# A 224-byte pad that moves h^T to the slots' place within 1024 bytes

## The chip, the core and the metric

One NeuronCore of a Trainium2 chip runs the whole program. The metric is the device time in microseconds. Three runs of the kernel before took 1566.57, 1566.58 and 1566.65 us, so the median is 1566.58 us. The engines are named as the profile names them: PE is TensorE's matmul and PEld its weight load, DVE is VectorE, ACT is ScalarE, POOL is GpSimd, SP is SyncE, which issues the transfers.

## What is computed

Two layers of a hybrid encoder over 512 tokens of width 1024, in float32. Cut to what matters here:

```
for l in range(2):
    h = rmsnorm(x, norm_pre[l])                     # 512 x 1024
    p = h @ w_in[l]                                 # 1024 x 10,400: q, k, v, gates of four mixers
    y_a, y_b, y_c, y_d = the four mixers of p       # windowed, recurrent, differential, latent attention
    g = sigmoid(p["gate"] + b_gate[l])              # 4 x 1024
    merged = sum(g_i * (y_i @ w_br_i[l]))           # four branch projections to width 1024
    x = x + rmsnorm(merged @ w_out[l], norm_post[l])
```

The product h @ w_in is by far the largest part. Its operand h is the same for all 10,400 columns.

## The kernel before

Every large product is made of three matmuls on float32r parts: each operand is split into a high part (a copy in float32r, made by ScalarE) and a low part (the rest, made by VectorE), and `mm3` (L434) issues high times high, high times low and low times high into one PSUM bank. A matmul has a stationary operand, which a weight load brings into the array, and a moving operand, which streams through it. In the profile's names a matmul `ps<-hTh,wl` has hTh moving and wl stationary.

h is transposed once per layer (L976, L977) into two tiles that hold it whole, hTh and hTl, each 128 partitions by 8 blocks by 512 tokens, that is 16,384 bytes in each partition, one block of 2048 bytes for each 128 channels. Nearly all columns of w_in go through `item_T` (L552): the weights are stationary (128 by 128), a block of hTh or hTl is moving (128 by 512 tokens). The rest goes through `item_tok` (L587) with the roles exchanged: 128 tokens of h stationary, 384, 416 or 512 columns of weights moving. The branch projections and w_out use the same functions with other tiles in the place of h (ya, yb, yc, yd and mh).

All those other tiles, the weights' parts (wh, wl) among them, are slots: 82 buffers of 2048 bytes in each partition, one pool, taken by `slot` (L380). The constants, the identity for transposes, h^T and a few small tiles lie in a pool of their own ahead of the slots, allocated one after the other in `setup` (L1708). Counted from the tiles' sizes, in bytes of each partition:

```
                    before            after
cst   (9232 B)        1152 =  1x1024+128     34144 = 33x1024+352
ident (512 B)        10400 = 10x1024+160     43392 = 42x1024+384
junk  (2048 B)       10912 = 10x1024+672     43904 = 42x1024+896
hTh   (16384 B)      13024 = 12x1024+736      1376 =  1x1024+352
hTl   (16384 B)      29408 = 28x1024+736     17760 = 17x1024+352
prm   (1024 B)       45792 = 44x1024+736     46016 = 44x1024+960
slots (82 x 2048 B)  47456 = 46x1024+352     48480 = 47x1024+352
```

A stationary piece of a slot starts 0, 512, 1024 or 1536 bytes into it. So before the change every operand pair of slots lies 0 or 512 bytes apart (counted within 1024), and every pair of h^T and a slot 384 or 896.

The order of the work is set by a planner in the kernel (`Sched`, L95, and `drive`, L1850), which keeps a modelled clock for each engine. Its rules read instruction shapes and tile names, never addresses; it prices a float32r matmul of 512 columns at 512/2400 + 0.0025 = 0.216 us (L187).

Of the kernel before, what the change touches and what calls it, by code (L numbers as in the profile page):

```python
# [9 lines left out]
F32 = mybir.dt.float32  # L10
F32R = mybir.dt.float32r
# [5 lines left out]
P = 128  # L17
# [23 lines left out]

N_SLOT = 82
N_STAGE = 4
W_FIRST = 8
BANKS = {"d": 3, "S": 2, "T": 2, "O": 1}
W_MIN = 7
# [316 lines left out]
class Trunk:  # L363
# [131 lines left out]
    def load_w(self, upto):  # L495
        nc = self.nc
        while self.w_dma < min(upto, len(self.specs)):
            src, a, b = self.specs[self.w_dma]
            if self.w_dma < W_FIRST:
                st = self.slot("st")  # L500
            else:
                st = self.stp.tile([P, 512], F32, tag="st", name=self.uid("st"))
                self.clk.take(st, "st", N_STAGE)
            v = st[:, :a * b].rearrange("p (a b) -> p a b", a=a)
# [9 lines left out]
    def pump(self, force=None):  # L514
        cls, self.clk.cls = self.clk.cls, "w"
        self.load_w(max(W_FIRST, self.w_split) + N_STAGE)
        n = 0
        while self.w_split < self.w_dma:
# [10 lines left out]
            del self.stage[i]  # L529
            if i < W_FIRST:  # L530
                self.rel(st)
                if i == W_FIRST - 1:
                    self.done.add("first")
            self.w_split += 1
            n += 1
        self.load_w(max(W_FIRST, self.w_split) + N_STAGE)
        self.clk.cls = cls
# [442 lines left out]
    def side_first(self):  # L980
        V = self.nc.vector
        yield ("n", 2 + 8 + 4 + 8 + W_FIRST)

# [16 lines left out]
        xs.append(self.load_x(self.I["x"], 3))  # L1000
        self.load_w(W_FIRST + N_STAGE)
        self.nc.sync.dma_start(self.cst, self.I["consts"][:, P:])
# [705 lines left out]
    def setup(self):  # L1708
        nc, I = self.nc, self.I
        V, S = nc.vector, nc.scalar  # L1710
        self.cst = self.cp.tile([P, K_END - P], F32, name="cst")
        self.ident = self.cp.tile([P, P], F32, name="ident")
        self.junk = self.cp.tile([P, 512], F32, name="junk")
        self.tiny_t = self.cp.tile([P, 1], F32, name="tiny")
        nc.gpsimd.memset(self.tiny_t, 1.0e-30)
        self.tiny = self.tiny_t[:, 0:1]
        self.eps_t = self.cp.tile([P, 1], F32, name="eps")
        nc.gpsimd.memset(self.eps_t, EPS)
        self.eps = self.eps_t[:, 0:1]
        self.hTh = self.cp.tile([P, 8, 512], F32R, name="hTh")  # L1720
        self.hTl = self.cp.tile([P, 8, 512], F32R, name="hTl")
        self.prm = self.cp.tile([P, 256], F32, name="prm")
        self.prm_h = self.cp.tile([P, P], F32, name="prmh")
        self.prm_d = self.cp.tile([P, 32], F32, name="prmd")
        self.clk.free_of_war = {self.junk.tensor.name}
        self.clk.by_block = {t.tensor.name for t in (self.hTh, self.hTl)}

# [97 lines left out]
    def run(self):  # L1825
# [6 lines left out]
        with tc.tile_pool(name="c", bufs=1) as self.cp, tc.tile_pool(name="s", bufs=N_SLOT) as self.sp, \  # L1832
                tc.tile_pool(name="st", bufs=N_STAGE) as self.stp, tc.tile_pool(name="sm", bufs=40) as self.smp, \
                tc.tile_pool(name="sw", bufs=6) as self.smw, \
# [147 lines left out]
```

## Time and profile before

| | before |
|---|---|
| median of three runs | 1566.58 us |
| profiled execution | 1567.27 us, span 1565.5 us |
| PE busy | 1550.1 us (99%) |
| PEld busy | 1257.3 us (80%) |
| DVE, ACT, POOL busy | 882.7, 734.8, 59.1 us |
| DMA | 136.34 MB, 87 GB/s over the span |
| granted clock | 0.997 over the span |

The profiled execution took 1.8 us more than its span, 0.7 us more than the median. A busy share of 99% does not tell how fast the matmuls come: they overlap, and a mean duration of 390 to 407 ns stands beside starts some 230 ns apart. What tells their pace is the distance from one start to the next, which is read from the timeline or from a window that holds nothing else and counts the instructions. Every instruction shows line L314, the planner's one place of issue, so the groups go by tile names.

### The profile page before, as it was taken

To read this page: it belongs to the slowest core of one execution; us is meant where nothing else is said; L and a number is where in the kernel's file an instruction comes from. 1 tells how busy PE (TensorE), PEld (TensorE's weight loads), DVE (VectorE), ACT (ScalarE), POOL (GpSimd) and SP (SyncE) were. 2 spreads that over 40 slices of the span, in tenths; PEclk is the share of its full clock that TensorE was granted. 3 is DMA by queue.
4 is the path that set the end of the run, shared out by engine and by line. 5 is a ranking of instruction groups with operands and counts; after the bars stand their busy time and mean duration, and the time that the engine had idled before them with its cause. 6 is when DMAs were issued, how large, how long until landed. Compare 5 with 4: busy or idle time off the path is not lost.

```text
span 1565.5 us, 21989 instructions
## 1 busy us (share of the span) xinstructions
PE 1550.1 (99%) x8024; PEld 1257.3 (80%) x8024; DVE 882.7 (56%) x1898; ACT 734.8 (47%) x1626; POOL 59.1 (4%) x254
## 2 busy tenths in 40 slices
PE   8999999999999999999999999999999999999998
PEld 7877888778787888888888878887787787788886
DVE  5698754446544453556657876544546445445553
ACT  5576653343444443443456765434435445334331
POOL 1300000000000100000010000000000001000000
PEclk9999999999999999999999999999999999999999
DMA  6422132223232333253252212232232223332521
GB/s 209 140 58 57 44 101 78 78 71 94 68 79 71 86 74 105 58 174 104 72 166 54 68 55 80 79 85 68 75 94 61 77 72 86 80 95 58 183 71 54
DMA packets 170884, 136.34 MB, mean 87 GB/s; under 512 B 25230, under 2 KB 158360, under 8 KB 170648
## 3 DMA queue, kind: packets, MB, share of 16 engines
q1 hardware_dynamic: 170776, 134.94, 31.1%
q8 instruction: 63, 1.03, 0.3%
q14 instruction: 45, 0.37, 0.1%
HBM read 129.45 MB, written 4.27 MB: 85 GB/s over the span
## 4 chain that ended last, share of the span: by engine, by line
PE 98%; DVE 1%; ACT 1%; DMA 0%; issue 0%; SPq 0%; DVEq 0%; ACTq 0%
PE ps L314 98%; DMA st<-in_w_in 0%; DVE rr L314 0%; SPq L314 0%; DVE hTl L314 0%; ACT hTh L314 0%; DVE rp L314 0%; ACT h L314 0%; DVE x L314 0%; ACT wh L314 0%; DVE wl L314 0%; ACT junk L314 0%; DVE h L314 0%; DVE xc L314 0%; DVE yb2l L314 0%
## 5 line engine op out<-in xcount | busy, mean ns | idle before, releaser
L314 PE MATMUL ps<-hTh,wh 128*128 128x512 f32 x1280 | 520.9, 407 | 0.7 <-DVE ud L314 0.7
L314 PE MATMUL ps<-hTh,wl 128*128 128x512 f32 x1280 | 505.8, 395 | 0.0
L314 PE MATMUL ps<-hTl,wh 128*128 128x512 f32 x1280 | 505.1, 395 | 0.0
L314 DVE TENSOR_TENSOR wl<-st,wh 128x512 fp32r<-128x512 f32 (+2 forms) x464 | 301.7, 666 | 278.5 <-ACT wh L314 276.9
L314 PEld LDWEIGHTS ps<-hTh,wh 128*128 128x128 f32 x1280 | 241.1, 188 | 65.8 <-issue 13.2
L314 PEld LDWEIGHTS ps<-hTh,wl 128*128 128x128 f32 x1280 | 240.9, 188 | 56.4
L314 ACT ACTIVATE wh<-st 128x512 fp32r<-128x512 f32 (+2 forms) x464 | 265.3, 606 | 43.9 <-DMA st<-in_w_in 37.4
L314 PEld LDWEIGHTS ps<-hTl,wh 128*128 128x128 f32 x1280 | 241.6, 189 | 49.2
L314 DVE CUSTOM_DVE_ANT_0 pC<-ps,cst 128x512 f32<-128x512 f32 x64 | 41.6, 688 | 83.4 <-PE ps L314 83.4
L314 PE MATMUL ps<-wh,hTh 128*128 128x416 f32 (+2 forms) x192 | 72.0, 375 | 0.7 <-ACT hTh L314 0.6
L314 PE MATMUL ps<-wl,hTh 128*128 128x416 f32 (+2 forms) x192 | 70.3, 366 | 1.5 <-DVE wl L314 1.5
L314 PE MATMUL ps<-wh,hTl 128*128 128x416 f32 (+2 forms) x192 | 70.3, 366 | 0.2
L314 ACT ACTIVATE pA<-pA,on 128x256 f32<-128x256 f32 x96 | 47.9, 501 | 38.4 <-DVE on L314 38.1
L314 ACT ACTIVATE pD<-ps,mx 128x512 f32<-128x512 f32 x48 | 32.9, 686 | 66.1 <-DVE mx L314 66.0
L314 ACT ACTIVATE pC<-pC,mx 128x512 f32<-128x512 f32 x64 | 45.8, 717 | 36.3 <-DVE mx L314 36.3
L314 DVE CUSTOM_DVE_ANT_0 pA<-ps,cst 128x256 f32<-128x256 f32 x96 | 36.0, 420 | 32.2 <-PE ps L314 32.2
L314 PE MATMUL ps<-wh,mh 128*128 128x512 f32 x128 | 50.0, 391 | 0.0
L314 PE MATMUL ps<-wh,ml 128*128 128x512 f32 x128 | 49.9, 390 | 0.0
L314 PE MATMUL ps<-wl,mh 128*128 128x512 f32 x128 | 49.9, 390 | 0.0
L314 ACT ACTIVATE wtC<-ps 128x512 f32<-128x512 f32 x32 | 19.0, 595 | 52.0 <-PE ps L314 52.0
L314 ACT ACTIVATE junk<-ps,rd 128x128 f32<-128x128 f32 x32 | 11.7, 365 | 65.1 <-DVE oC L314 64.4
L314 DVE TENSOR_REDUCE mx<-ps 128x1 f32<-128x512 f32 x48 | 32.7, 686 | 14.7 <-PE ps L314 14.5
(390 smaller groups left out, 2210.7 us busy)
## 6 DMA issues: line engine op xcount, KB each, us to landing
st<-in_w_in SPq DMA_DIRECT2D x216, 256.0 KB
st<-in_w_in SPq DMA_DIRECT2D x240, 128.0 KB
st<-in_w_out SPq DMA_DIRECT2D x32, 256.0 KB
x<-in_x SPq DMA_DIRECT2D x16, 256.0 KB
st<-in_w_br_c SPq DMA_DIRECT2D x16, 256.0 KB
x<-x SPq DMA_DIRECT2D x16, 256.0 KB
st<-in_w_in SPq DMA_DIRECT2D x16, 208.0 KB
st<-in_w_in SPq DMA_DIRECT2D x16, 192.0 KB
```

The costliest lines, as they stand in the source:

```text
L314: op.fn(*op.a, **op.k)
```

## The change

In `setup`, h^T's two tiles are allocated first, behind a pad of 56 float32 (224 bytes); the constants and the small tiles follow; a second pad of 200 float32 (800 bytes) closes the pool. The pads together are 1024 bytes, so the slots keep their place within 1024 bytes, and h^T now has the same one. The pads are never read or written.

```diff
+PAD = (56, 200)
...
     def setup(self):
         nc, I = self.nc, self.I
         V, S = nc.vector, nc.scalar
+
+        self.cp.tile([P, PAD[0]], F32, name="pad0")
+        self.hTh = self.cp.tile([P, 8, 512], F32R, name="hTh")
+        self.hTl = self.cp.tile([P, 8, 512], F32R, name="hTl")
         self.cst = self.cp.tile([P, K_END - P], F32, name="cst")
         self.ident = self.cp.tile([P, P], F32, name="ident")
         self.junk = self.cp.tile([P, 512], F32, name="junk")
...
-        self.hTh = self.cp.tile([P, 8, 512], F32R, name="hTh")
-        self.hTl = self.cp.tile([P, 8, 512], F32R, name="hTl")
         self.prm = self.cp.tile([P, 256], F32, name="prm")
         self.prm_h = self.cp.tile([P, P], F32, name="prmh")
         self.prm_d = self.cp.tile([P, 32], F32, name="prmd")
+        self.cp.tile([P, PAD[1]], F32, name="pad1")
```

No instruction is added, removed or moved: on each of the five engines the built program has the same instructions in the same order (6802 rows on PE, 1849 on DVE, 1313 on ACT, 247 on POOL, 581 on SP), and only running numbers in tile names and the line numbers differ. What changes is where operands lie.

## Rows read from the trace of the kernel before

**Rows 1.** Page, parts 1, 2 and 4: engines, granted clock, chain.
```profile
PE 1550.1 (99%) x8024; PEld 1257.3 (80%) x8024; DVE 882.7 (56%) x1898; ACT 734.8 (47%) x1626; POOL 59.1 (4%) x254
PEclk9999999999999999999999999999999999999999
PE 98%; DVE 1%; ACT 1%; DMA 0%; issue 0%; SPq 0%; DVEq 0%; ACTq 0%
```

**Rows 2.** Waits of TensorE, longest first: total us, times, longest us.
```profile
PE ps L314 <- DVE h L314: 4.0, 3, 1.9
PE ps L314 <- DVE wl L314: 1.5, 2, 1.0
```

**Rows 3.** Windows, four unbroken runs: length, each engine's busy us (instructions), clock.
```profile
core 0: us, PE busy (x) PEld busy (x) DVE busy (x) ACT busy (x) POOL busy (x), PEclk, DMA share, GB/s
706.48:717.66 11.18, 11.18 (x49) 9.01 (x48) 5.07 (x9) 3.42 (x7) 0.00 (x0) 1.00 0.28 94
717.67:721.76 4.09, 4.09 (x20) 3.38 (x18) 2.50 (x4) 2.12 (x4) 0.00 (x0) 1.00 0.38 115
732.96:741.12 8.16, 8.16 (x37) 6.75 (x36) 6.49 (x11) 4.04 (x7) 0.00 (x0) 1.00 0.30 96
741.13:762.88 21.75, 21.75 (x97) 17.98 (x96) 12.41 (x29) 8.10 (x18) 0.00 (x0) 1.00 0.24 76
```

**Rows 4.** Timeline of TensorE, short runs' first rows: start us, us, engine, line.
```profile
207.60 0.40 PE L314 MATMUL ps<-hTh,wh 128*128 128x512 f32 x1
210.40 0.39 PE L314 MATMUL ps<-yb0h,wh 128*128 128x512 f32 x1
212.46 0.60 PE L314 MATMUL ps<-ident,pD 128*128 128x128 f32 x4
...
229.91 0.40 PE L314 MATMUL ps<-yb0h,wh 128*128 128x512 f32 x1
231.31 0.49 PE L314 MATMUL ps<-ident,pD 128*128 128x128 f32 x3
```

**Rows 5.** Instructions on hTh: count, shortest, median, longest ns, first to last start.
```profile
L314 PE MATMUL ps<-hTh,wl x1280: 387/393/405, 37.4 to 1506.4; 128*128 128x512 f32 x183
L314 PEld LDWEIGHTS ps<-hTh,wl x1280: 186/188/193, 37.2 to 1506.2; 128*128 128x128 f32 x183
```

**Rows 6.** Groups of TensorE's matmuls: count, busy us, mean ns, idle before.
```profile
L314 PE MATMUL ps<-hTh,wh 128*128 128x512 f32 x1280 | 520.9, 407 | 0.7 <-DVE ud L314 0.7
L314 PE MATMUL ps<-hTh,wl 128*128 128x512 f32 x1280 | 505.8, 395 | 0.0
L314 PE MATMUL ps<-hTl,wh 128*128 128x512 f32 x1280 | 505.1, 395 | 0.0
L314 PE MATMUL ps<-wl,mh 128*128 128x512 f32 x128 | 49.9, 390 | 0.0
L314 PE MATMUL ps<-yb0l,wh 128*128 128x512 f32 x16 | 6.3, 394 | 0.0
...
L314 PE MATMUL ps<-wh,hTl 128*128 128x384 f32 x64 | 21.6, 338 | 0.0
L314 PE MATMUL ps<-ukvh,cTl 128*128 128x384 f32 x8 | 2.7, 335 | 0.0
L314 PE MATMUL ps<-wh,hTl 128*128 128x512 f32 x64 | 25.2, 394 | 0.0
```

**Rows 7.** Groups of 128-column matmuls, and of the 96-row pairs.
```profile
L314 PE MATMUL ps<-ident,pD 128*128 128x128 f32 x192 | 28.8, 272 | 0.1
L314 PE MATMUL ps<-cv,wtC 128*128 128x128 f32 x256 | 34.1, 276 | 0.0
L314 PE MATMUL ps<-ktl,qth 96*128 96x512 f32 x48 | 19.0, 395 | 0.0
```

**Rows 8.** Windows where VectorE is busiest.
```profile
60.00:200.00 140.00, 139.84 (x715) 115.84 (x714) 113.90 (x197) 93.79 (x192) 0.00 (x0) 1.00 0.23 61
790.00:1000.00 210.00, 206.93 (x1046) 171.24 (x1046) 150.57 (x278) 126.15 (x266) 7.45 (x35) 1.00 0.29 79
```

## Prediction

> **What bounds the kernel now.** I read the page first: PE is busy 99% of the span, and the chain that ended last is PE for 98% at full clock [rows 1]. The reader is to see there that nothing but PE's own pace can move this time by more than a few microseconds. Next come PE's waits: the longest kind sums to 4.0 us over the run, and on split weights PE waited twice, 1.5 us in all [rows 2]. So the order feeds PE in time. The question left is how far apart two matmuls start. The change touches no instruction, only places, so I looked for rows that already show matmuls whose two operands lie as h^T and the weights will lie: any pair of slots, which are 0 or 512 bytes apart within 1024. The windows over unbroken runs show it. A run of h^T matmuls has 48 weight loads in 11.18 us, 232.9 ns each; the branch projections, same code, same weights' tiles, slots in the place of h^T, take 4.09 us for 18 (227.2 ns) and 8.16 us for 36 (226.7 ns); w_out takes 21.75 us for 96 (226.6 ns) [rows 3]. Clock is 1.00 in all four, DVE and ACT are busy in each. The pace changes at the tile, not at a later time: the second window begins where the first ends.
>
> **What else could make the difference.** DMA moves 76 GB/s beside the w_out run, 94 beside h^T's, 115 beside the first projection run [rows 3], and the first and the last of these are both at 227. I took the start-to-start distances of all float32r matmuls of 512 columns and 128 rows from the trace (h^T's lie between the rows of [rows 5], 1280 of that kind, 3840 in all with the other two kinds [rows 6]). Distances under 260 ns: h^T moving or stationary 3639, mean 232.6; slot pairs 1099, mean 228.2. With ACT and DVE both idle beside the matmul h^T's mean is 233.0 and the slots' 227.3, with both busy 232.8 and 229.4. So neighbours don't explain it. Nor does the region of the memory: 960 h^T blocks and 30 slots as moving operand lie in the same 16 KB (bytes 32,768 to 49,151), with medians 232 and 227. What is left is the place within some smaller unit, or the distance between the two operands in it; after the change both equal those of slot pairs.
>
> **The change part by part.** (1) h^T as moving operand, 3840 matmuls. Not each gains the whole 6 ns, since slot pairs reach their flat pace only after some matmuls: in a run of nine after h^T, 2.06 us or 228.9 ns each; in a run of six, 1.40 us or 233.3 ns, no better than the twelve of h^T ahead of the nine, 2.80 us or 233.3 ns [rows 4]. So I split the distances by place in an unbroken run (counted again at each change of kind, stall or other shape). First four: h^T 232.1 (1044 of them), slots 231.2. Fifth to twelfth: 232.7 (1286), slots 227.8. Later: 232.9 (1309), slots 226.7. Gain: 1044 x 0.9 + 1286 x 4.9 + 1309 x 6.2 ns = 0.9 + 6.3 + 8.1 = 15.3 us. These include the stationary h^T at 512 columns. From groups alone the bounds are: mean durations 395 for h^T against 394 for the worst branch row and 390 for w_out [rows 6], that is 1 to 5 ns x 3840 = 3.8 to 19.2 us; from the windows, 6.3 ns x 3840 = 24.2 us [rows 3]. I take 15.3, because the branch runs stand among the same side work as h^T's runs. The starts over 260 ns (172 with h^T, a wait for a semaphore in front; they lift the first group's mean to 407 [rows 6]) I leave as they are.
>
> (2) h^T as stationary operand, 384 and 416 columns, 384 matmuls: 338 ns against 335 in the nearest slot group [rows 6], 3 ns x 384 = 1.2 us; bounds 0 and 6 ns x 384 = 2.3 us. I take 1.2.
>
> (3) The identity moves from 160 to 384 within 1024, while the slots that it meets stay at 352. It is the moving operand of 690 transposes of 128 columns, whose largest group stands in [rows 7]. No row has this pair of places. The nearest are 272 ns for the identity now and 276 for slot pairs of the same width [rows 7]: 4 ns x 690 = 2.8 us either way. I take 0, the row it is nearest to.
>
> (4) Constants, junk and parameters are read and written by ACT, DVE, POOL and DMA alone, all off the chain [rows 1]. Cost 0; PE's lead hides them. If a DVE operation on the mask tables took 10 ns more, 160 of them would be 1.6 us of DVE, with 44% of DVE idle. The pads cost nothing: no instruction names them.
>
> (5) What comes late next: with PE faster by 1%, the engines behind it have 1% less time. DVE is busiest at 113.90 of 140 us and 150.57 of 210 us [rows 8], still 81% and 72%, and the order was planned for 216 ns per matmul, which is faster than any run here. I charge 0.5 us for waits that grow, bounds 0 and 2.
>
> Sum: -15.3 - 1.2 + 0 + 0.5 = -16.0 us. The profiled execution has span 1565.5 and time 1567.27; it becomes 1549.5 and 1551.3. The median is 0.7 us below it: 1566.6 - 16.0 = **1550.6 us**. With each term at its ends: -24.2 - 2.3 - 2.8 = -29.3 (1537) and -3.8 + 0 + 2.8 + 2 = +1.0 (1568); the ends of term 1 are the unlikely ones, and without them -21 to -12 is what I expect of this case, 1545 to 1555.
>
> The skill has a rule that speaks against all this. On two starts side by side the rows show 232.9 and 226.6 ns by tile [rows 3]. The Trainium skill, "SBUF — State Buffer", section "Who interferes with whom", says that TensorE has two independent read ports, one for the moving operand and one for weight loads, that PE never waits on anyone, and that only the port pair shared by VectorE and GpSimd contends. By that rule addresses cannot matter, and the sum is 0. The trace does not agree: POOL is at 0.00 in all four windows and the pace still differs by tile.
>
> **The rivals.** *No change.* The 6 ns belong to h^T's tiles for a reason that the move leaves: their 16,384 bytes each, or their low place ahead of the slots. For: no row shows h^T at any other place. Against: its blocks are read 2048 bytes at a time as slots are, and the shared 16 KB above. Then only terms 3 and 5 act: 1566.6, 1563.5 to 1569. That is the result that the rule of the Trainium skill named above would have.
>
> *Part of it.* The flat pace is reached only where a run is long; if h^T's runs, cut by scores and transposes, reach it later than the branch runs do, only the 1309 late ones gain: 8.1 + 0.6 = 8.7 us, 1558. For: the 96-row pairs of slots have 395 ns, as h^T has [rows 7], and never settle. Against: the projections settle after 4 matmuls in most runs.
>
> *PE no longer the bound.* DVE, at 81% between 60 and 200 us and 72% between 790 and 1000 [rows 8], takes the gain of these 350 us: a loss of 350/1565 of 16.0, some 4 us, 1554. Against: two waits for split weights in the whole run [rows 2].
>
> *Slower.* Same place means same cell of the memory: a moving block that starts where its weights start could collide with them at each load. Price: the same 6 ns with the other sign, 6 x 3639 = +22 us, 1588; it decides from the point where the mean distance of h^T's matmuls rises over 232.6. For: the short run of slots at 233.3 [rows 4]. Against: 150 loads of slot pairs at 227 in [rows 3], half of them 0 bytes apart within 1024.
>
> **How the numbers follow.** Forecast (1545 to 1555 by itself) 0.78; part of it, or PE no longer the bound, 0.10 (1554 to 1560); no change 0.07; slower 0.05. The likeliest gives 1550.6. Range 1542 to 1560: it holds the forecast with an allowance for longer flat runs, and the partial cases. What a measurement can tell from no change is about 0.2%, 3.1 us. Faster by more: 0.78 + 0.10 = 0.88. Within: 0.07. Slower: 0.05.
>
> **What would show it.** In the profile of the changed kernel, windows over long h^T runs should hold a load per 226 to 228 ns, the groups hTh,wl and hTl,wh should fall from 395 to 391 or 392, the branch and w_out groups should stay at 390 to 394, and PE's waits should stay under 12 us in all. h^T groups at 395 with the time unchanged would prove the place innocent. h^T at 391 with a smaller gain than 12 us would put the loss in PE's waits or in the transposes (over 274).

## The result and the profile after

The changed kernel takes 1549.49 us (median of 4 runs, 1548.76 to 1550.06) against 1566.62 us before (4 runs, 1566.57 to 1567.01): ratio 0.989, 95% interval 0.9873 to 0.9907, 17.1 us less. Forecast were 1550.6 us and a range of 1542 to 1560.

The first thing to read in the new profile is whether PE is still what bounds, and whether any other engine did other work. The page of the changed kernel, parts 1 and 2:

```profile
span 1548.3 us, 21989 instructions
PE 1533.6 (99%) x8024; PEld 1256.1 (81%) x8024; DVE 882.6 (57%) x1898; ACT 734.9 (47%) x1626; POOL 61.2 (4%) x254
PEclk8999999999999999999999999999999999999999
```

Counts are those of before, DVE and ACT have the same busy time within 0.1 us, and the row of the granted clock differs from that of before in the first of its 40 slices alone, 8 for 9 [rows 1]; term 2 below comes back to it. The span is 17.2 us shorter, and all of it is PE's. The same four runs of matmuls as in [rows 3], in the changed kernel (length, then busy us and instructions of PE, PEld, DVE, ACT, POOL, then clock, DMA share, GB/s): h^T, branch projection of 18, branch projection of 36, w_out.

```profile
698.53:709.40 10.87, 10.87 (x49) 9.01 (x48) 5.08 (x9) 3.42 (x7) 0.00 (x0) 1.00 0.30 96
709.41:713.47 4.06, 4.06 (x19) 3.38 (x18) 2.48 (x4) 2.11 (x4) 0.00 (x0) 1.00 0.37 113
724.38:732.52 8.14, 8.14 (x37) 6.75 (x36) 6.49 (x11) 4.04 (x7) 0.00 (x0) 1.00 0.31 97
732.53:754.28 21.75, 21.75 (x97) 17.97 (x96) 12.41 (x29) 8.10 (x18) 0.00 (x0) 1.00 0.24 76
```

The first row is what the change is about: 48 weight loads in 10.87 us, 226.5 ns each, where they took 11.18 us. w_out, 96 in 21.75 us, is as it was to the hundredth. DVE and ACT do the same work in the h^T window as before (5.08 and 3.42 us), DMA moves as much. So h^T's matmuls now have the pace of pairs of slots. The groups that answer to [rows 6 and 7]:

```profile
L315 PE MATMUL ps<-hTh,wh 128*128 128x512 f32 x1280 | 515.8, 403 | 1.1 <-DVE ud L315 1.1
L315 PE MATMUL ps<-hTh,wl 128*128 128x512 f32 x1280 | 499.7, 390 | 0.0
L315 PE MATMUL ps<-hTl,wh 128*128 128x512 f32 x1280 | 499.5, 390 | 0.0
L315 PE MATMUL ps<-wl,mh 128*128 128x512 f32 x128 | 49.8, 389 | 0.0
L315 PE MATMUL ps<-wh,hTl 128*128 128x512 f32 x64 | 25.0, 390 | 0.0
L315 PE MATMUL ps<-wh,hTl 128*128 128x384 f32 x64 | 21.5, 336 | 0.0
L315 PE MATMUL ps<-wh,hTl 128*128 128x416 f32 x64 | 23.9, 373 | 0.1
L315 PE MATMUL ps<-ident,pD 128*128 128x128 f32 x192 | 28.8, 272 | 0.1
```

The three large groups fall by 4 or 5 ns each, and the last two of them now have the mean of w_out's (the first holds the starts behind a wait). Only the 416-column group rises, by 8 ns. PE's waits, the answer to [rows 2] (total us, times, longest), did not grow:

```profile
PE ps L315 <- DVE h L315: 2.8, 3, 1.1
PE ps L315 <- DVE wl L315: 1.6, 2, 1.0
PE ps L315 <- DVE ud L315: 1.1, 1, 1.1
```

### The profile page after: what moved, and what is told of

The parts are those of the page before. It is cut to its first block, busy times and chain, and to the rows that moved or that the text cites. A ratio compares the mean times of both kernels' runs of the same rounds, so it can differ in the third digit from the quotient of the medians.

```text
span 1548.3 us, 21989 instructions
## 1 busy us (share of the span) xinstructions
PE 1533.6 (99%) x8024; PEld 1256.1 (81%) x8024; DVE 882.6 (57%) x1898; ACT 734.9 (47%) x1626; POOL 61.2 (4%) x254
## 4 chain that ended last, share of the span: by engine, by line
PE 95%; DVE 2%; ACT 2%; DMA 1%; issue 1%; SPq 0%; DVEq 0%; ACTq 0%
PE ps L315 95%; DMA st<-in_w_in 1%; DVE wl L315 0%; ACT wh L315 0%; ACT lg L315 0%; DVE lg L315 0%; DVE rr L315 0%; DMA x<-x 0%; DVE x L315 0%; SPq L315 0%; DVE xc L315 0%; DVE hTl L315 0%; ACT hTh L315 0%; DVE rp L315 0%; ACT h L315 0%
## 5 line engine op out<-in xcount | busy, mean ns | idle before, releaser
L315 PE MATMUL ps<-hTh,wl 128*128 128x512 f32 x1280 | 499.7, 390 | 0.0
L315 PE MATMUL ps<-hTl,wh 128*128 128x512 f32 x1280 | 499.5, 390 | 0.0
L315 PEld LDWEIGHTS ps<-wh,hTh 128*128 128x128 f32 x192 | 37.0, 193 | 5.5 <-ACT hTh L315 1.1
```

The lines of the kernel that those rows point to most:

```text
L315: op.fn(*op.a, **op.k)
```

## The experiments

My theory at this point: what counts is the distance between a matmul's two operands within some unit of memory. Rivals: the absolute place (352 is good, 736 is bad); being first in the pool, or the constants' new home; and for the size of the unit everything up to 1024 bytes. Twelve kernels were run, each timed against the kernel before (1566.9 to 1567.2 us in these series).

**1. h^T first in the pool, but at its old place within 1024.** Undoes the place; the order of the tiles stays as in the changed kernel, and the constants move 384 bytes further with h^T.

```diff
-PAD = (56, 200)
+PAD = (152, 104)
```

> The changed kernel with a first pad of 608 bytes instead of 224 (and a last one of 416): h^T still ahead of the constants, but at 736 within 1024, 384 from the slots, as in the kernel before. My theory (the distance between the two operands within some unit up to 1024 bytes sets the pace): h^T's matmuls of 512 columns start 232 to 233 ns apart again, groups at 395 ns, and the time is that of before, 1565 to 1569 us. Rival (being first in the pool, or the constants' new place, gave the gain): 227 to 228 ns and 1548 to 1551 us.

Measured: 1566.79 us, ratio 1.0 (0.999 to 1.0009); h^T's groups are back at 394 and 395, here the first of them.

```profile
L315 PE MATMUL ps<-hTh,wl 128*128 128x512 f32 x1280 | 505.6, 395 | 0.0
```

The whole gain is gone with 384 bytes of pad. Order in the pool and the constants' home are worth nothing.

**2. The slots moved instead, h^T untouched.** In the kernel before:

```diff
         self.prm_d = self.cp.tile([P, 32], F32, name="prmd")
+        self.cp.tile([P, 96], F32, name="pad1")
```

> The kernel before with nothing moved but the slots: a pad of 384 bytes at the end of the constants' pool puts them at 736 within 1024, where h^T is. Constants and h^T stay where they were. Theory of the distance: h^T's matmuls at 227 to 228 ns, 1547 to 1551 us, although h^T wasn't touched. Rival (352 within 1024 is a good place by itself, 736 a bad one): h^T's matmuls stay at 232 to 233 ns and the slot pairs rise from 228 to 232 or 233, so 1568 to 1576 us.

Measured: 1548.92 us, ratio 0.988 (0.9865 to 0.9894). The windows of this kernel over a run of h^T and over the branch projection of 36:

```profile
696.05:706.92 10.87, 10.87 (x49) 9.01 (x48) 5.08 (x9) 3.43 (x7) 0.00 (x0) 1.00 0.28 96
721.89:730.04 8.15, 8.15 (x37) 6.75 (x36) 6.50 (x11) 4.04 (x7) 0.00 (x0) 1.00 0.31 97
```

48 loads in 10.87 us again, with h^T and every constant at the addresses of before. The absolute place falls as a cause of the gain: both operands at 736 are as fast as both at 352.

**3. Both moved by 128 bytes.** `PAD = (88, 200)`.

> The changed kernel with a first pad of 352 bytes, so h^T and the slots both lie at 480 within 1024, 128 further than in the changed kernel and still 0 apart. Theory of the distance: 227 to 228 ns and 1548 to 1551 us. Rival (the absolute place, 352, does it): both kinds of pairs slow, 232 ns and more, 1568 to 1576 us.

Measured: 1549.35 us, ratio 0.9883 (0.9866 to 0.9899), groups at 390. A third common place, the same pace.

**4. Distance 512.** `PAD = (184, 72)`.

> The changed kernel with a first pad of 736 bytes: h^T at 864 within 1024, 512 from the slots' start. Pairs of slots are 0 or 512 apart and both are fast, so if the distance counts within 512 bytes or less, this is as fast as the changed kernel: 227 to 228 ns, 1548 to 1551 us. If it is the same start within 1024 that counts (the tiles' starts, not the pieces'), h^T's matmuls go back to 232 to 233 ns and 1565 to 1569 us.

Measured: 1548.76 us, ratio 0.988 (0.9865 to 0.9894), groups at 390. The unit is 512 bytes or a divisor of it.

**5 to 12. The other distances.** The slots stay at 352; the first pad gives h^T's distance, the second fills up to 1024 bytes: `PAD = (56 + d/4, 200 - d/4)` for a distance of d bytes.

> The changed kernel with h^T 256 bytes further than the slots within 1024 (608), slots at 352. The distances of 0 and 512 are fast, 384 and 896 slow. If the unit is 256 bytes or a divisor of it, this is fast: 227 to 228 ns, 1548 to 1551 us. If the unit is 512 bytes, it is slow: 232 to 233 ns, 1565 to 1569 us. I hold the two to be equally likely.

> The changed kernel with h^T 128 bytes further than the slots (480 against 352); its pieces are 128 or 640 apart, the mirror image of before, 384 and 896. Theory that the distance counts whichever operand lies ahead: slow, 232 to 233 ns, 1565 to 1569 us. If only a moving operand behind its weights is slow, fast, 1548 to 1551 us.

> The changed kernel with h^T 64 bytes further than the slots (416 against 352). If any distance but 0 within the unit is slow: 232 to 233 ns, 1565 to 1569 us. If 64 bytes lie in the same row of the unit and rows of 128 bytes count: 227 to 228 ns, 1548 to 1551 us. A value between would say that the cost grows with the distance.

> The changed kernel with h^T 32 bytes further than the slots (384 against 352). As for 64 bytes: if any distance but 0 is slow, 232 to 233 ns and 1565 to 1569 us; if only distances of 128 bytes or more count, 227 to 228 ns and 1548 to 1551 us; between these, it grows with the distance.

> The changed kernel with h^T 192 bytes further than the slots (544 against 352), which is 64 bytes short of the next multiple of 256. At 64 the h^T matmuls took a middle pace where h^T was moving (229.7 ns) and the slow one where it was stationary (233.2). Theory that the distance counts within 256 bytes, from the stationary to the moving operand: here the two change places, so h^T moving is slow, 232 to 233 ns, h^T stationary at 229 to 230, and the time is 1564 to 1569 us. Rival (64 bytes either way are alike): 229.7 ns and 1555 to 1559 us.

> The changed kernel with h^T 224 bytes further (576 against 352), 32 short of a multiple of 256. Both signs of 32 appear already in the run at 32, h^T moving at 233.2 ns and stationary at 233.0, so the theory of the distance expects both at 233 again and 1565 to 1570 us. Rival (it isn't the distance but h^T's own start, some starts being good): anything from 1548 to 1570.

> The changed kernel with h^T 96 bytes further (448 against 352). Between 64 (229.7 ns, 1557 us) and 128 (232.6 ns, 1567 us): if the pace goes evenly with the distance, 231 ns and 1560 to 1564 us; if 32 bytes past a multiple of 64 is the bad case, 233 ns and 1566 to 1570 us.

> The changed kernel with h^T 160 bytes further (512 against 352), which is 96 short of a multiple of 256. If h^T moving and stationary change places between 96 and 160 as the theory of the distance says, this run's stationary h^T has the pace that the moving one has at 96, and the other way round. In us 1560 to 1570. A place better than 0 would show here or at 96: under 226.5 ns and under 1547 us; I give that 1 in 20.

All in one table. The last two columns are the mean distance, where it is under 260 ns, from the start of a 512-column matmul to the start of the next one of that shape, with h^T moving (3463) and with h^T stationary (176), counted from each trace's start times.

| h^T behind the slots by | time us | ratio to before (95%) | h^T moving ns | h^T stationary ns |
|---|---|---|---|---|
| 0 (changed kernel) | 1549.49 | 0.989 (0.9873 to 0.9907) | 228.1 | 227.9 |
| 32 | 1568.55 | 1.0012 (1.0002 to 1.0021) | 233.2 | 232.9 |
| 64 | 1557.3 | 0.994 (0.9924 to 0.9956) | 229.7 | 233.4 |
| 96 | 1570.0 | 1.0016 (1.0007 to 1.0026) | 233.5 | 233.8 |
| 128 | 1566.93 | 1.0001 (0.9991 to 1.001) | 232.6 | 232.5 |
| 160 | 1572.77 | 1.0034 (1.0021 to 1.0047) | 234.0 | 233.6 |
| 192 | 1568.79 | 1.0009 (1.0 to 1.0018) | 233.3 | 229.8 |
| 224 | 1568.56 | 1.0012 (1.0002 to 1.0021) | 233.1 | 232.9 |
| 256 | 1548.89 | 0.9884 (0.9866 to 0.9901) | 228.1 | 227.7 |
| 384 (before) | 1566.62 | 1 | 232.6 | 232.5 |
| 384 (experiment 1) | 1566.79 | 1.0 (0.999 to 1.0009) | 232.6 | 232.5 |
| 512 | 1548.76 | 0.988 (0.9865 to 0.9894) | 228.1 | 228.0 |

256 is as good as 0 and 512, and 384 is as slow as 128: of the two units that I held equally likely, it is 256 bytes. Within it the sign of the distance counts. At 64 the moving h^T has a middle pace and the stationary one the slow pace; at 192, where a stationary h^T lies 64 bytes ahead of a multiple of 256, the two change places, as expected. The groups of these two kernels show it, first at 64, h^T moving and then stationary:

```profile
L315 PE MATMUL ps<-hTh,wl 128*128 128x512 f32 x1280 | 503.0, 393 | 0.0
L315 PE MATMUL ps<-hTl,wh 128*128 128x512 f32 x1280 | 500.2, 391 | 0.0
L315 PE MATMUL ps<-wh,hTl 128*128 128x512 f32 x64 | 25.3, 395 | 0.0
```

and at 192, the same three groups in the profile's order:

```profile
L315 PE MATMUL ps<-hTh,wl 128*128 128x512 f32 x1280 | 505.5, 395 | 0.0
L315 PE MATMUL ps<-hTl,wh 128*128 128x512 f32 x1280 | 505.2, 395 | 0.0
L315 PE MATMUL ps<-wh,hTl 128*128 128x512 f32 x64 | 25.0, 391 | 0.0
```

Between 96 and 160 the figures differ by 0.5 ns at most, too little to show the change of places by itself, and the time at 160, 1572.77 us, lies above the 1560 to 1570 that I expected. The value between the two paces at 64 does not say that the cost grows with the distance, as I had thought it would: 32 is slower than 64. The expectation at 96 of an even growth (231 ns) was wrong too: 32, 96, 160 and 224 are all at 233 to 234. No distance beat 0, 256 or 512, and the four kernels with these in other homes (experiments 2 to 5) lie at 1548.76 to 1549.35 us with intervals that overlap the changed kernel's: there is no better version among them. The worst, 160, has this window over the run of 48 h^T matmuls:

```profile
707.58:718.81 11.23, 11.23 (x49) 9.04 (x48) 5.07 (x9) 3.42 (x7) 0.00 (x0) 1.00 0.29 93
```

234.0 ns a load. From 1548.76 to 1572.77 us, 24 us or 1.5%, by pads that nothing reads.

## Why the prediction was right, step by step

**What bounds.** Right: the gain is PE's start-to-start distance and nothing else. Summing these distances by class from first to last start (before, after): 512 columns with h^T 959.6 and 942.3 us, -17.4; 512 columns of slots 333.6 and 332.9, -0.7; transposes 75.9 and 75.2, -0.7; other 128-column matmuls 94.6 and 95.3, +0.7; 384 columns with h^T 35.75 and 35.57, -0.2; 416 columns 42.2 and 43.3, +1.1 (differences taken before rounding). That is -17.2, the 17.2 us of the span.

**Term 1, h^T with 512 columns**, forecast 15.3 us. Under 260 ns the mean went from 232.6 to 228.1 over the same 3639: 16.5 us. By place in a run: the first four 232.1 to 230.5, the fifth to twelfth 232.7 to 227.5, later 232.9 to 226.7, that is 1.7 + 6.7 + 8.1. The late ones hit the forecast exactly; the early ones gained 1.2 us more. The reason can be seen on the slots: their own first four fell from 231.2 to 229.2 ns and their mean from 228.2 to 227.5 (0.8 us over 1099). It is the 141 starts right behind an h^T run that did it, 230.9 to 227.3 ns, and the other 164 moved little, 231.3 to 230.8; in experiment 1, with h^T slow again, the two are back at 230.7 and 231.3. So the slow starts of slot runs, my yardstick for h^T, were in part an aftermath of the h^T run ahead of them. Taking them as undisturbed made the term too small, and left the slots' own gain out.

**Term 2, 384 and 416 columns**, forecast 1.2 us of gain, was the step that failed: 0.2 us gained at 384 and 1.1 us lost at 416. One slot group of 8 matmuls was a thin yardstick: at 384 columns the mean under 260 ns fell by some 2 ns, at 416 by 0.4. The loss at 416 comes from TensorE's granted clock, which the term left out. In both executions it falls to 0.50, its level of 1.2 GHz, where these matmuls begin and behind PE's first waits for h, and it stays there for 6.8 us before and for 10.2 us after. These are the two windows on PE alone (length, busy us and instructions, clock, DMA share, GB/s):

```profile
12.32:19.14 6.82, 6.23 (x20) 0.50 1.04 366
10.18:20.41 10.23, 9.12 (x28) 0.50 1.06 390
```

In them a 416-column matmul mostly starts 347 ns ahead of the next, outside them some 190. Of the 192 with h^T, 12 run there, whole or in part, before and 20 after. Against 190 ns each that cost 3.3 us before and 4.5 us after, 1.2 us more, about the whole loss. Of the others, 11 starts in each kernel are over 260 ns, and the mean duration of the group shown above is 354 ns in both. So the group does not follow the distance between operands but the length of the low stretch: it stood at 365 ns before,

```profile
L314 PE MATMUL ps<-wh,hTl 128*128 128x416 f32 x64 | 23.4, 365 | 0.2
```

and has 373 in the changed kernel, 354 in experiment 2 (no low stretch there), 358 in 4 (3.4 us of it), 370 in 3 (3.4 us in each layer) and 373 in 5 (10.2 us), all with the fast pace at 512 columns. Why the clock stays low for longer in one execution than in another is open.

**Term 3, the identity**, forecast 0: the group is at 272 before and after, and the distance from a transpose to the next start, where under 260 ns, is 102.6 ns before and 102.7 after. Of their class the transposes of h took 1.3 us less, which is PE's shorter wait for h (4.0 to 2.8 us in all), and those of pD 0.5 us more.

**Term 4, the constants**, forecast 0: DVE 882.7 and 882.6 us, ACT 734.8 and 734.9; and experiment 2 has the gain with the constants unmoved, experiment 1 has none with the constants moved.

**Term 5, waits that grow**, 0.5 us charged: not needed, PE's waits on other engines fell from 7.9 to 7.2 us.

**The sum.** That it came out within 1.1 us of the forecast is in part luck. The 512-column matmuls of h^T and of the slots gave 18.1 us where 15.3 were forecast, and term 2 missed by 2.1 us the other way, 0.9 us lost where 1.2 of gain were forecast.

**The rivals.** *No change* fell with the result, and its two reasons with experiments 1 and 2: h^T is slow again at the front of the pool, and fast in its old home when the slots come to it. The Trainium skill, "SBUF — State Buffer", section "Who interferes with whom", gives TensorE two independent read ports and says that it never waits on anyone; the trace does not agree: in the h^T windows, with POOL at 0.00, the same matmuls start 226.5 ns apart at distance 0 and 232.9 at 384 [rows 3]. The measurement decides, and here PE's pace depends on where its own two operands lie. *Part of it* was refuted by the fifth to twelfth matmuls, which gained 5.2 ns each. *PE no longer the bound*: it is still 99% busy. *Slower* had the wrong place: not the same start but 160 bytes of distance costs, 5.8 us by the times.

**What stays open.** Which two reads meet. While a matmul streams its moving operand, the array loads the next one's weights: in [rows 5] a load takes 188 ns beside matmuls 233 ns apart. In nearly every pair of this kernel the next weights lie at the same distance as the own ones, so these runs can't tell whether it is the own or the next weights that count. Where a run of slots meets a run with h^T stationary they do differ, but the 14 starts of each trace there were slow in both orders before (means 233.2 and 232.2 ns) and fast in both after (227.4 and 228.0), which doesn't decide it. That reads of both operands collide in a unit of 256 bytes was not shown; shown is that the distance within 256 bytes sets the pace. That the common place does not matter was tried at distance 0 alone (352, 736 and 480); at every other distance the slots lay at 352. Distances under 32 bytes were not tried.

## What to carry to other kernels

Where PE is the bound and its matmuls come slower than others of the same shape in the same trace, compare where their operands lie before looking for waits: a pad of a few hundred bytes, at equal instructions, was worth 1.1% here. Give the large tiles that meet in float32r matmuls of 512 columns the same start within 256 bytes, and count afresh whenever a small tile is added to a pool ahead of them; at 384 and 416 columns the gain was small. When one kind of work is the yardstick for another, check that it isn't itself disturbed by what stands ahead of it. Before a group's mean is compared across two executions, look at where the granted clock was low in each.

## What the runs showed of the hardware that I had not expected

The unit of 256 bytes, and that the sign counts: 64 bytes from the stationary to the moving operand cost a moving h^T 1.6 ns a matmul over the best, 64 the other way 5.2 ns. That 160 bytes cost more than the 384 of the kernel before, 1.4 ns a matmul and 5.8 us in all. And a floor that no place lowers: late in a run (from the thirteenth matmul) the mean of slot pairs is 226.7 ns in all fourteen traces, and that of h^T at distances 0, 256 and 512 is the same. The Trainium skill, "TensorE: Matmul & The Clock Gate", section "Back-to-back issue gap", gives 512/2.4 + 2.5 = 215.8 ns as the isolated gap of a matmul of 512 columns and about 131 ns as the sustained spacing of pairs of a weight load and a matmul. No run here reaches either with these float32r pairs. The matmuls with 96 rows (95 distances before, 233.8 ns, and 94 after, 233.9), though both their operands are slots 0 or 512 bytes apart, kept the slow pace in the changed kernel; what slows them was not tried.
